# Strassen products for ff tiles 16 to 19 in the feed-forward blocks of a decoder layer, on one Trainium2 core

## The chip, the cores and the metric

One core of one Trainium2 chip runs the whole kernel. The metric is device microseconds of one execution. TensorE (PE) does the matmuls; its weight loads (PEld) run beside them. VectorE (DVE), ScalarE (ACT) and GpSimd (POOL) do the elementwise work, SyncE (SP) issues most DMAs. Each engine takes its own instructions in order and waits for the others at semaphores.

## What is computed

One decoder layer on 512 tokens of width 1024, all in float32: a feed-forward block, a token mixer of three attention kinds, and a second feed-forward block. Each of them takes an RMS-normalised input. The change touches the feed-forward blocks (FFN 1 and FFN 2) alone:

```python
def swiglu(x, w_gate, w_up, w_down):
    return (jax.nn.silu(x @ w_gate) * (x @ w_up)) @ w_down

x = x + 0.5 * swiglu(rms_norm(x, ffn1_norm[i]), ffn1_w_gate[i], ffn1_w_up[i], ffn1_w_down[i])
x = x + token_mixer(rms_norm(x, mix_norm[i]), w_in[i], ...)
x = x + 0.5 * swiglu(rms_norm(x, ffn2_norm[i]), ffn2_w_gate[i], ffn2_w_up[i], ffn2_w_down[i])
```

The inner width D_FF is 2816, which is 22 ff tiles of 128.

## The kernel before

**Products in parts.** Every float32 operand is split into a high part in the matmul's own number format (ACT, a copy) and a low part, the rest (DVE or POOL, a subtraction). A product is three matmuls: high x high, high x low, low x high (`mm3`, L502). For weights the two parts are `whi` (L106, ACT) and `wlo` (L107). A matmul streams 512 columns.

**Weights.** `Weights` (L61) holds a list of loads (`specs`) and a list of halves to be split (`plan`), in order of use. `get` splits up to the half that is asked for. `bg`, called once for each step of work, splits the half two places ahead of the current one. `sub` is the engine that does `wlo`: DVE in the feed-forward blocks. After the last half of a load is split, the load two further on is issued on SP. Split halves live in four rotating buffers, or in tiles of their own where `W.held` (L397) names them.

**Gate and up.** `ffn` (L564) runs 11 steps p, each for two ff tiles (2p and 2p+1): g0, g1 (gate), u0, u1 (up). Each of these is 24 matmuls (`mm_in`). Gate results go through tanh on ACT and into `m` on DVE (`act_g`), up results are multiplied to `a` on DVE (`act_u`).

**Down, as Strassen products.** For ff tiles 0 to 15, four tiles (512 rows of `w_down`) make a block. Block c's left operands come from the steps 2c and 2c+1 (`left_blocks`): four quarter sums on POOL for the second tile of a pair, split on ACT and DVE after the next gate or up half (`split_sums`: `sh` and `sl`, then one more split of half that size). Block c's seven products are made in steps 2c+2 and 2c+3, one behind each gate or up half (`down_block`): 12 matmuls each, into one PSUM bank of each of two kinds, and added on DVE into the residual x (`add_x`, L644), each bank at one or two places. The right operands come from `Blocks` (L127): two loads of 1 MB, a sum on POOL ahead of the first product and one behind each of the splits 1 to 4; the splits' `wlo` of these seven are always POOL's. The next block is loaded when part 6 is split.

**Down, plain.** ff tiles 16 to 21 are split as they are (`ah`, `al`). In step 10 tiles 16 and 17 (`d4`) come between gate and up: 48 matmuls. After step 10 the tail multiplies tiles 18 to 21 (`d5_0`, `d5_1`): for each of four token tiles two halves of 12 matmuls, each added into x (`down_tile`).

**The tail of FFN 1** carries the norm of the mixer in three stages over the following token tiles (`Stages`, `tick`): square and sum on ACT, a power on POOL (`pow`, the operation `nr1..r`, L519), `h` on DVE in two halves (L534: x times `pow` times gain), eight transposes on PE (`nt`, L543), and their split into `hmh` (ACT) and `hml` (DVE). In a tick the transposes and split of tile t-1 are issued ahead of the square of tile t. `W.bg(4)` in each round splits one of the four parts c0.0 to c1.1 (128 x 912) of the first mixer weights. The c tile (24 matmuls of 456 columns) follows on PE. The tail of FFN 2 has no norm; it writes each half tile of the output (256 KB) through SP.

Of the kernel before, what the change touches and what calls it, by code (L numbers as in the profile page):

```python
# [12 lines left out]
F32R = mybir.dt.float32r  # L13
# [7 lines left out]
NT = SEQ // 128  # L21
# [212 lines left out]
def drain(g):  # L234
    for _ in g:
        pass
# [8 lines left out]
def hybrid_trunk_kernel(ctx: ExitStack, tc: tile.TileContext, x, rel_bias, ffn1_norm, ffn1_w_gate, ffn1_w_up,  # L245
# [3 lines left out]
    nc = tc.nc  # L249
# [24 lines left out]
    def t4(name, dt=F32):  # L274
        return big.tile([128, 1024], dt, tag="t4", name=name)

    def t4k(name):
        return t4(name, F32R).rearrange("p (k t) -> p k t", k=2)
# [9 lines left out]
    specs, plan, blocks = [], [], {}  # L288

    def add_spec(loads, parts, name, planned=True):  # L290
        specs.append((loads, parts, name))
        if planned:
            plan.extend((name, p) for p in range(len(parts)))

    def cols(w, name, c0, planned=True):

        def view(raw):
            return raw.rearrange("p (k c) -> p k c", k=8)
        add_spec([(view, w[:, c0:c0 + 256].rearrange("(k p) c -> p k c", p=128))],
                 [lambda raw, g=g: view(raw)[:, :, g * 128:g * 128 + 128] for g in range(2)], name, planned)  # L300
# [8 lines left out]
    def rows(w, name, r0, nk, c0, nc_):  # L309

        src = w[r0:r0 + nk * 128, c0:c0 + nc_].rearrange("(k p) c -> p k c", p=128)
        loads = [(lambda raw: raw[:, :nk * nc_].rearrange("p (k c) -> p k c", k=nk), src)]
        parts = [lambda raw, h=h: raw[:, :nk * nc_].rearrange("p (k c) -> p k c", k=nk)
                 [:, h * nk // 2:(h + 1) * nk // 2, :] for h in range(2)]
        add_spec(loads, parts, name)

    def ffn_specs(f):
        wg, wu, wd = ffn_w[f]
        for c in range(4):
            src = wd[c * 512:c * 512 + 512].rearrange("(k p) c -> p k c", p=128)  # L320
            blocks[f"w{f}{c}"] = Blocks(
                nc, lambda h, c=c: big2.tile([128, 4, 512], F32, tag="hT", name=f"raww{f}{c}{h}"),
                lambda c=c: t4(f"rawe{f}{c}").rearrange("p (k c) -> p k c", k=2),
                [src[:, :, h * 512:h * 512 + 512] for h in range(2)],
                lambda c=c: c < 3 and blocks[f"w{f}{c + 1}"].load())
        for p in range(11):
            between = p in range(2, 10)
            cols(wg, f"g{f}{p}", 256 * p, not between)
            if p == 10:
                rows(wd, f"d{f}4", 16 * 128, 2, 0, 1024)  # L330
            cols(wu, f"u{f}{p}", 256 * p, not between)
            if between:
                for i, (kind, j) in enumerate((("g", 0), ("g", 1), ("u", 0), ("u", 1))):
                    plan.append((f"{kind}{f}{p}", j))
                    if p % 2 * 4 + i < 7:
                        plan.append((f"w{f}{p // 2 - 1}", p % 2 * 4 + i))
        for h in range(2):
            rows(wd, f"d{f}5_{h}", (18 + 2 * h) * 128, 2, 0, 1024)

    ffn_specs(0)  # L340
    def c_view(raw):
# [52 lines left out]
        rows(w_out, f"wo{n}", 256 * n, 2, 0, 1024)  # L394
    ffn_specs(1)
    W = Weights(nc, rawp, wsp, specs, plan, blocks, 2)
    W.held, W.held_tile = [(n, p) for n in ("d05_0", "d15_0", "wo2", "c0") for p in range(2)], lambda name: t4(name, F32R)  # L397


    xt = [t4(f"x{t}") for t in range(NT)]  # L400
# [101 lines left out]
    def mm3(ps, terms):  # L502

        n = len(terms)
        for i, (lh, ll, rh, rl) in enumerate(terms):
            for q, (l, r) in enumerate(((lh, rh), (lh, rl), (ll, rh))):
                nc.tensor.matmul(ps, l, r, start=i == 0 and q == 0, stop=i == n - 1 and q == 2)  # L507
                if q == 2 or ps.shape[1] == 512:
                    yield ps.shape[1] * (1 if ps.shape[1] == 512 else 3) / 2400
# [37 lines left out]
    def hk(hT, k, s):  # L547
        return hT[k // 4][0][:, k % 4, s], hT[k // 4][1][:, k % 4, s]

    ALL = slice(0, SEQ)  # L550

    def tok(t):
        return slice(t * 128, (t + 1) * 128)
# [10 lines left out]
    def ffn(f, hT, order, hooks, after_tile):  # L564
# [3 lines left out]
        def mm_in(kind, p, j, ps, s):  # L568
            wh, wl = W.get(f"{kind}{f}{p}", j)
            for k, _ in enumerate(mm3(ps[:, s], [(wh[:, k, :], wl[:, k, :]) + hk(hT, k, s) for k in range(KD)])):  # L570
                if p == 10 and kind == "u" and k % 12 == 0 or p and k == 0:
                    W.bg(4 if p == 10 else 2)

        def act_g(ff, g):
            th = tmp.tile([128, 512], F32, tag="z", name=f"th{f}{ff}")
# [5 lines left out]
        def act_u(ff, m, u):  # L581
            a = tmp.tile([128, 512], F32, tag="p", name=f"a{f}{ff}", bufs=6)
            nc.vector.tensor_tensor(a, m, u, op=ALU.mult)  # L583
            if ff < 16:
                left_blocks(ff, a)
                return
            if ff % 2 == 0:
                aT[ff // 2, "pair"] = (t4k(f"ah{f}{ff}"), t4k(f"al{f}{ff}"))
            pair = aT[ff // 2, "pair"]
            aT[ff] = (pair[0][:, ff % 2, :], pair[1][:, ff % 2, :])  # L590
            split(aT[ff][0], aT[ff][1], a)
# [41 lines left out]
        def down_block(c, i):  # L633

            w = W.get(f"w{f}{c}", i)
            W.bg()
            for u in range(2):
                ps = (mm, sc)[u](f"dn{f}{c}{i}{u}")
                drain(mm3(ps, [left(c, pr, i, u) + (w[0][:, pr, :], w[1][:, pr, :]) for pr in range(2)]))
                for hr, hc, sign in INTO[i]:  # L640
                    add_x(ps, 2 * hr + u, HALVES[hc], sign)
# [4 lines left out]
        def down_tile(t, k0, parts, hook=None):  # L646
            for half in range(2):
                ps = sc(f"dn{f}{k0}{half}{t}")
                csl = slice(512 * half, 512 * half + 512)
                terms = []  # L650
                for k, w in enumerate(parts):
                    ah, al = aT[k0 + k]
                    terms.append((ah[:, tok(t)], al[:, tok(t)], w[0][:, 0, csl], w[1][:, 0, csl]))
                drain(mm3(ps, terms))
                if half == 0 and hook is not None:
                    hook()
                add_x(ps, t, csl)

        for p in range(11):
            ps, ms = {}, {}  # L660
            step = 0
            if p == 1:
                blocks[f"w{f}0"].load()
            W.cap = W.first[f"u{f}0", 1] if p == 0 else 1 << 30
            todo = order if p == 0 else [("g", 0, ALL), ("g", 1, ALL), None, ("u", 0, ALL), ("u", 1, ALL)]
            for item in todo:
                if item is None:
                    if p == 10:
                        parts = [W.get(f"d{f}4", k) for k in range(2)]
                        for t in range(NT):  # L670
                            if t % 2 == 0:
                                W.bg()
                            down_tile(t, 16, parts)
                    continue
                if callable(item):
                    item()
                    continue
                kind, j, s = item
                if (kind, j) not in ps:
                    ps[kind, j] = (mm if kind == "g" else sc)(f"{kind}{f}{p}{j}")  # L680
                mm_in(kind, p, j, ps[kind, j], s)
                while late:
                    late.pop()()
                if p == 0 and s.stop == SEQ:
                    W.cap += 1
                    W.split(W.cap)
                if s.stop == SEQ:
                    if kind == "g":
                        ms[j] = act_g(2 * p + j, ps["g", j])
                    else:  # L690
                        act_u(2 * p + j, ms[j], ps["u", j])
                if p in range(2, 10):
                    if p % 2 * 4 + step < 7:
                        down_block(p // 2 - 1, p % 2 * 4 + step)
                    step += 1
            if p in hooks:
                hooks[p]()
        parts = [W.get(f"d{f}5_{k // 2}", k % 2) for k in range(4)]
        for t in range(NT):
            down_tile(t, 18, parts, nstage.tick)  # L700
            after_tile(t)
            nstage.tick()
            W.bg(4)


    nstage = Stages()
# [18 lines left out]
    def u_part(f, p):  # L725
# [4 lines left out]
    order = [n0(1, 2), n0(0, 3), ("g", 0, lo2), n0(2, 2), n0(1, 3), u_part(0, 0), ("g", 1, lo2), n0(2, 3), u_part(0, 1),  # L730
             ("u", 0, lo2)] + rest
# [683 lines left out]
    for n in range(2):  # L1415
        parts = [W.get(f"wo{n}", p) for p in range(2)]
# [3 lines left out]
    parts = [W.get(f"wo{2 + k // 2}", k % 2) for k in range(4)]  # L1420
# [45 lines left out]
```

## Time and profile before

| | |
|---|---|
| runs | 1292.51, 1290.85, 1292.12 us |
| median | 1292.12 us |
| the profiled execution | 1292.1 us |
| its span, first to last instruction | 1290.0 us |
| mean granted clock of TensorE | 0.994 of full speed |
| PE busy in the span | 99% |

The profile is of one execution. A row of a timeline tells when an instruction (or several alike in a row, x2) began and how long it took; in brackets stands how long its engine had been idle and what released it. An operation that has begun but cannot get its operands counts as running. The ends of matmuls are modelled, so the distance of two starts is the better measure of one.

### The profile page before, as it was taken

To read this page: it belongs to the slowest core of one execution; us is meant where nothing else is said; L and a number is where in the kernel's file an instruction comes from. 1 tells how busy PE (TensorE), PEld (TensorE's weight loads), DVE (VectorE), ACT (ScalarE), POOL (GpSimd) and SP (SyncE) were. 2 spreads that over 40 slices of the span, in tenths; PEclk is the share of its full clock that TensorE was granted. 3 is DMA by queue.
4 is the path that set the end of the run, shared out by engine and by line. 5 is a ranking of instruction groups with operands and counts; after the bars stand their busy time and mean duration, and the time that the engine had idled before them with its cause. 6 is when DMAs were issued, how large, how long until landed. Compare 5 with 4: busy or idle time off the path is not lost. (4 is left out here: it accounts for less than half of the span.)

```text
span 1290.0 us, 17385 instructions
## 1 busy us (share of the span) xinstructions
PE 1273.0 (99%) x6880; PEld 1081.7 (84%) x6880; DVE 798.7 (62%) x1377; ACT 484.1 (38%) x872; POOL 475.8 (37%) x313
## 2 busy tenths in 40 slices
PE   9999999999999999999999999999999999999998
PEld 8888888888889889889887778888898888888887
DVE  4467777765573766597854554446645767676553
ACT  4242333332243555454556432224233333333220
POOL 2475757561011444446440000000015756666500
PEclk9999999999999999999989999999999999999999
DMA  5424141422433222222221034433332233333131
GB/s 196 141 69 139 57 162 37 161 69 82 137 126 96 60 81 79 87 66 83 66 83 46 33 103 147 131 96 101 98 108 89 98 99 102 112 108 103 66 98 66
DMA packets 101779, 125.08 MB, mean 97 GB/s; under 512 B 3817, under 2 KB 85225, under 8 KB 101698
## 3 DMA queue, kind: packets, MB, share of 16 engines
q1 hardware_dynamic: 96690, 114.08, 27.2%
q10 hardware_dynamic: 3456, 5.24, 1.3%
q0 software_dynamic: 1552, 4.65, 1.1%
q8 instruction: 54, 0.88, 0.3%
q14 instruction: 27, 0.22, 0.1%
HBM read 119.13 MB, written 4.84 MB: 96 GB/s over the span
## 5 line engine op out<-in xcount | busy, mean ns | idle before, releaser
L107 DVE TENSOR_TENSOR wlo<-raw,whi 128x1024 fp32r<-128x1024 f32 (+1 forms) x146 | 219.7, 1510 | 61.3 <-ACT whi L106 61.0
L106 ACT ACTIVATE whi<-raw 128x1024 fp32r<-128x1024 f32 (+1 forms) x178 | 185.5, 1050 | 64.8 <-PE u L507 26.5
L644 DVE SCALAR_TENSOR_TENSOR x<-dn,x 128x512 f32<-128x512 f32 x224 | 143.4, 682 | 30.0 <-PE dn L507 27.5
L107 POOL TENSOR_TENSOR wlo<-raww,whi 128x1024 fp32r<-128x1024 f32 x40 | 99.5, 2487 | 96.6 <-ACT whi L106 96.6
L583 DVE TENSOR_TENSOR a<-m,u 128x512 f32<-128x512 f32 x44 | 30.2, 687 | 101.8 <-PE u L507 101.8
L107 POOL TENSOR_TENSOR wlo<-raw,whi 128x1024 fp32r<-128x1024 f32 x32 | 76.7, 2395 | 29.0 <-ACT whi L106 25.1
L576 ACT ACTIVATE th<-g 128x512 f32<-128x512 f32 x44 | 26.2, 595 | 143.2 <-PE g L507 143.1
L507 PE MATMUL gt<-rmh,wlo 128*128 128x512 f32 x192 | 76.2, 397 | 0.0
L507 PE MATMUL gt<-rml,whi 128*128 128x512 f32 x192 | 76.0, 396 | 0.0
L507 PE MATMUL gt<-rmh,whi 128*128 128x512 f32 x192 | 76.0, 396 | 0.0
L507 PE MATMUL g<-hah,whi 128*128 128x512 f32 (+1 forms) x192 | 71.6, 373 | 0.2 <-ACT hah L512 0.2
L507 PE MATMUL g<-hal,whi 128*128 128x512 f32 (+1 forms) x192 | 71.4, 372 | 0.3 <-DVE hal L513 0.3
L507 PE MATMUL g<-hah,wlo 128*128 128x512 f32 (+1 forms) x192 | 71.4, 372 | 0.1
L507 PE MATMUL u<-hbh,wlo 128*128 128x512 f32 (+1 forms) x192 | 71.4, 372 | 0.0
L507 PE MATMUL u<-hah,wlo 128*128 128x512 f32 (+1 forms) x192 | 71.4, 372 | 0.0
L507 PE MATMUL g<-hbh,whi 128*128 128x512 f32 (+1 forms) x192 | 71.4, 372 | 0.0
L507 PE MATMUL u<-hah,whi 128*128 128x512 f32 (+1 forms) x192 | 71.4, 372 | 0.0
L507 PE MATMUL u<-hbh,whi 128*128 128x512 f32 (+1 forms) x192 | 71.4, 372 | 0.0
L507 PE MATMUL g<-hbl,whi 128*128 128x512 f32 (+1 forms) x192 | 71.3, 372 | 0.0
L507 PE MATMUL g<-hbh,wlo 128*128 128x512 f32 (+1 forms) x192 | 71.3, 371 | 0.0
L507 PE MATMUL u<-hbl,whi 128*128 128x512 f32 (+1 forms) x192 | 71.3, 371 | 0.0
L507 PE MATMUL u<-hal,whi 128*128 128x512 f32 (+1 forms) x192 | 71.3, 371 | 0.0
(1111 smaller groups left out, 3493.3 us busy)
## 6 DMA issues: line engine op xcount, KB each, us to landing
raw<-in_w_in SPq DMA_DIRECT2D x25, 1024.0 KB, 5.1
raw<-in_ffn_w_gate SPq DMA_DIRECT2D x22, 1024.0 KB, 5.1
raw<-in_ffn_w_up SPq DMA_DIRECT2D x22, 1024.0 KB, 5.2
raww<-in_ffn_w_down SPq DMA_DIRECT2D x16, 1024.0 KB, 6.1
raw<-in_ffn_w_down SPq DMA_DIRECT2D x6, 1024.0 KB, 5.0
raw<-in_w_in SPq DMA_DIRECT2D x8, 512.0 KB, 4.5
raw<-in_w_out SPq DMA_DIRECT2D x4, 1024.0 KB, 4.9
x<-in_x SPq DMA_DIRECT2D x4, 512.0 KB, 6.2
```

Of the source, the lines that this page charges most:

```text
L106: nc.scalar.activation(h, src, AF.Copy)
L107: sub.tensor_tensor(l, src, h.bitcast(F32), op=ALU.subtract)
L507: nc.tensor.matmul(ps, l, r, start=i == 0 and q == 0, stop=i == n - 1 and q == 2)
L576: nc.scalar.activation(th, g, AF.Tanh, scale=0.5)
L583: nc.vector.tensor_tensor(a, m, u, op=ALU.mult)
L644: nc.vector.scalar_tensor_tensor(xt[t][:, csl], ps, 0.25 * sign, xt[t][:, csl], op0=ALU.mult, op1=ALU.add)
```

## The change

The four ff tiles 16 to 19 become a fifth Strassen block. Its left operands come from steps 8 and 9 as with the other blocks; its seven products all fall into step 10, two behind g0, two behind g1, two behind u0 and one behind u1 (`products`). The plan lists the halves in that order. `d4` and its 48 matmuls go away, and the tail multiplies ff tiles 20 and 21 alone, 6 matmuls for each half of a token tile. Fewer tiles are held apart: `d5` is split into the rotating buffers. `mm_in` calls `bg` once in every step, also in the tenth. While the tail runs, `W.sub` is POOL, so that the parts c0.0 to c1.1 are split there; behind the tail it is DVE again.

```diff
+    def products(p, i):
+
+        if p == 10:
+            return range(2 * i, min(2 * i + 2, 7))
+        return range(p % 2 * 4 + i, min(p % 2 * 4 + i + 1, 7))
+
     def ffn_specs(f):
         wg, wu, wd = ffn_w[f]
-        for c in range(4):
+        for c in range(5):
...
-                lambda c=c: c < 3 and blocks[f"w{f}{c + 1}"].load())
+                lambda c=c: c < 4 and blocks[f"w{f}{c + 1}"].load())
         for p in range(11):
-            between = p in range(2, 10)
+            between = p > 1
             cols(wg, f"g{f}{p}", 256 * p, not between)
-            if p == 10:
-                rows(wd, f"d{f}4", 16 * 128, 2, 0, 1024)
             cols(wu, f"u{f}{p}", 256 * p, not between)
             if between:
                 for i, (kind, j) in enumerate((("g", 0), ("g", 1), ("u", 0), ("u", 1))):
                     plan.append((f"{kind}{f}{p}", j))
-                    if p % 2 * 4 + i < 7:
-                        plan.append((f"w{f}{p // 2 - 1}", p % 2 * 4 + i))
-        for h in range(2):
-            rows(wd, f"d{f}5_{h}", (18 + 2 * h) * 128, 2, 0, 1024)
+                    plan.extend((f"w{f}{p // 2 - 1}", q) for q in products(p, i))
+        rows(wd, f"d{f}5", 20 * 128, 2, 0, 1024)
...
-    W.held, W.held_tile = [(n, p) for n in ("d05_0", "d15_0", "wo2", "c0") for p in range(2)], lambda name: t4(name, F32R)
+    W.held, W.held_tile = [(n, p) for n in ("wo2", "c0") for p in range(2)], lambda name: t4(name, F32R)
...
-                if p == 10 and kind == "u" and k % 12 == 0 or p and k == 0:
-                    W.bg(4 if p == 10 else 2)
+                if p and k == 0:
+                    W.bg()
...
-            if ff < 16:
+            if ff < 20:
                 left_blocks(ff, a)
...
-            todo = order if p == 0 else [("g", 0, ALL), ("g", 1, ALL), None, ("u", 0, ALL), ("u", 1, ALL)]
+            todo = order if p == 0 else [("g", 0, ALL), ("g", 1, ALL), ("u", 0, ALL), ("u", 1, ALL)]
             for item in todo:
-                if item is None:
-                    if p == 10:
-                        parts = [W.get(f"d{f}4", k) for k in range(2)]
-                        for t in range(NT):
-                            if t % 2 == 0:
-                                W.bg()
-                            down_tile(t, 16, parts)
-                    continue
...
-                if p in range(2, 10):
-                    if p % 2 * 4 + step < 7:
-                        down_block(p // 2 - 1, p % 2 * 4 + step)
+                if p > 1:
+                    for q in products(p, step):
+                        down_block(p // 2 - 1, q)
                     step += 1
...
-        parts = [W.get(f"d{f}5_{k // 2}", k % 2) for k in range(4)]
+        parts = [W.get(f"d{f}5", k) for k in range(2)]
+        W.sub = nc.gpsimd
         for t in range(NT):
-            down_tile(t, 18, parts, nstage.tick)
+            down_tile(t, 20, parts, nstage.tick)
             after_tile(t)
             nstage.tick()
             W.bg(4)
+        W.sub = nc.vector
```

## Rows read from the trace of the kernel before

**Rows 1.** The page: the span, and its part 1 (busy us, share of the span, instructions of each engine).
```profile
span 1290.0 us, 17385 instructions
PE 1273.0 (99%) x6880; PEld 1081.7 (84%) x6880; DVE 798.7 (62%) x1377; ACT 484.1 (38%) x872; POOL 475.8 (37%) x313
```
**Rows 2.** The chain that ended last, in order of time (start us, us, what), its last 75 us: a `down_block` product of step 9, the two plain ff tiles in the middle of step 10, the tail of FFN 2, the last add.
```profile
1215.37 2.72 PE dn L507 x12
1242.57 10.88 PE dn L507 x48
1264.33 21.83 PE dn L507 x96
1286.17 0.69 DVE x L644
```
**Rows 3.** Timeline of PE around the tail of FFN 1 (start us, us, engine, line, operation, out<-in, count [idle before <-releaser]): the first matmul of the tail, the transposes `nt` of tiles 0 to 2, the first matmul of the c tile, and a weight load of the c tile that waited.
```profile
344.74 0.39 PE L507 MATMUL dn<-whi,ah 128*128 128x512 f32 x1
355.63 1.03 PE L543 MATMUL nt<-ident,h 128*128 128x128 f32 x8
361.96 1.03 PE L543 MATMUL nt<-ident,h 128*128 128x128 f32 x8
368.30 1.03 PE L543 MATMUL nt<-ident,h 128*128 128x128 f32 x8
369.09 0.45 PE L507 MATMUL c<-whi,hmh 128*128 128x456 f32 x1
373.10 0.19 PEld L507 LDWEIGHTS c<-wlo,hmh 128*128 128x128 f32 x1 [0.22 <-DVE wlo L107]
```
**Rows 4.** Timelines of DVE, ACT and POOL in the tail of FFN 1 (columns as above): `a` and `ah` of ff tile 21; the last add of token tile 0 and its `pow`; `whi`, `pow`, `wlo` and `h` of token tile 1.
```profile
344.94 0.69 DVE L583 TENSOR_TENSOR a<-m,u 128x512 f32<-128x512 f32 x1 [0.74 <-PE u L507]
345.67 0.63 ACT L512 ACTIVATE ah<-a 128x512 fp32r<-128x512 f32 x1 [2.91 <-DVE a L583]
350.38 0.69 DVE L644 SCALAR_TENSOR_TENSOR x<-dn,x 128x512 f32<-128x512 f32 x1 [2.03 <-PE dn L507]
352.52 0.56 POOL L519 TENSOR_TENSOR nr10r<-nr10v,neghalf 128x1 f32<-128x1 f32 x1 [52.52 <-DVE nr10v L517]
358.27 0.97 ACT L106 ACTIVATE whi<-raw 128x912 fp32r<-128x912 f32 x1
358.65 0.55 POOL L519 TENSOR_TENSOR nr11r<-nr11v,neghalf 128x1 f32<-128x1 f32 x1 [5.57 <-DVE nr11v L517]
359.27 1.11 DVE L107 TENSOR_TENSOR wlo<-raw,whi 128x912 fp32r<-128x912 f32 x1 [0.70 <-ACT whi L106]
360.30 1.41 DVE L534 SCALAR_TENSOR_TENSOR h<-x,nr11r,gain 128x512 f32<-128x512 f32 x2
```
**Rows 5.** DMA issues, from the page's part 6 and from the last 26 us (out<-in, queue, count, KB each, median us from issue to landing).
```profile
raww<-in_ffn_w_down SPq DMA_DIRECT2D x16, 1024.0 KB, 6.1
out_x<-x SPq DMA_DIRECT2D x8, 256.0 KB, 2.0
```
**Rows 6.** Timelines of DVE and POOL at two places (columns as above): in the mixer a pair of `work` operations alone and one with a POOL split, then 10 us of FFN 2 in step 7.
```profile
438.14 1.34 DVE L1070 SCALAR_TENSOR_TENSOR work<-rl,cw,work 128x384 f32<-128x384 f32 x2 [0.68 <-ACT rl L1069]
446.95 3.28 DVE L1070 SCALAR_TENSOR_TENSOR work<-rl,cw,work 128x384 f32<-128x384 f32 x2 [0.77 <-ACT rl L1069]
447.29 2.52 POOL L107 TENSOR_TENSOR wlo<-raw,whi 128x1024 fp32r<-128x1024 f32 x1
1140.19 2.40 POOL L107 TENSOR_TENSOR wlo<-raww,whi 128x1024 fp32r<-128x1024 f32 x1
1140.45 3.22 DVE L107 TENSOR_TENSOR wlo<-raw,whi 128x1024 fp32r<-128x1024 f32 x1
1142.54 3.38 POOL L150 TENSOR_TENSOR raww<-raww,raww 128x1024 f32<-128x1024 f32 x1
1143.59 3.42 DVE L513 TENSOR_TENSOR sl<-sum,sh 128x1024 fp32r<-128x1024 f32 x1
1146.31 2.95 POOL L107 TENSOR_TENSOR wlo<-raww,whi 128x1024 fp32r<-128x1024 f32 x1 [0.38 <-ACT whi L106]
1146.93 2.88 DVE L513 TENSOR_TENSOR a<-a,a 128x512 fp32r<-128x512 f32 x1
```
**Rows 7.** The chain in order of time and the timelines of DVE, POOL and ACT at the start of step 8 in FFN 2, where products of the third block begin.
```profile
1169.12 5.44 PE g L507 x24
1169.77 1.22 DVE L107 TENSOR_TENSOR wlo<-raw,whi 128x1024 fp32r<-128x1024 f32 x1
1169.93 2.35 POOL L600 TENSOR_TENSOR sum<-a,a 128x256 f32<-128x256 f32 x2 [1.31 <-DVE a L583]
1173.00 1.06 ACT L512 ACTIVATE sh<-sum 128x1024 fp32r<-128x1024 f32 x1 [5.92 <-POOL sum L600]
1173.05 0.74 POOL L600 TENSOR_TENSOR a<-a,a 128x256 f32<-128x256 f32 x1
```
**Rows 8.** PE in four stretches of 3.4 us (stretch: us, PE busy us (matmuls), granted clock as a share of full speed, DMA share, GB/s).
```profile
571.46:574.87 3.41, 1.82 (x13) 1.00 0.47 166
574.87:578.29 3.42, 3.42 (x19) 0.50 0.02 5
687.51:690.93 3.42, 2.06 (x17) 1.00 0.14 40
690.93:694.34 3.41, 3.41 (x25) 1.00 0.00 0
```

## Prediction

> **What bounds the kernel now.** I read the page first: PE is busy 1273.0 of 1290.0 us, DVE 62%, ACT 38%, POOL 37% [rows 1]. Then the chain in order of time: its last 75 us are PE without a hole, a `down_block` product (12 matmuls) taking 2.72 us, so 0.2267 us a matmul [rows 2]. A matmul less is worth that, as long as nothing else becomes late. So I read, engine by engine, the two places where the change shortens PE's work between two dependent steps: the last gate and up step, and the loop over four token tiles behind it. In FFN 1 that loop carries the next norm: 344.74 to 369.09 is 24.35 us for 4 x 24 matmuls (21.76) and 3 x 8 transposes (0.79 each), 24.13 us of work [rows 3]. PE waits 0.2 us there, but the norm is only just in time: the second half of `h` of tile 1 ends at 360.30 + 1.41 = 361.71, its transposes start at 361.96 [rows 3, 4].
>
> **1. Matmuls.** Before, the four ff tiles cost 48 matmuls (10.88 us) in the middle of step 10 and half of the 96 at the end (21.83 us) [rows 2]. After it there are 7 products x 12 = 84 and a tail of 48: 132 for 144. 12 x 0.2267 = 2.72 us less per FFN, **-5.44 us** for two.
>
> **2. Work beside PE.** Per FFN there are 24 + 8 adds into x for 16: 16 x 0.69 = 11 us more on DVE; POOL gets 7 splits and 5 sums of 2.4 us and 10 sums of 0.74 us, some 36 us in a step of 38 us. Most of it has room: a product's four adds take 2.7 us, and PSUM has three buffers for each kind. As bare time I cost it at nothing. The loads are 3 MB either way (two 1 MB loads of block 4 for `d4` and half of `d5`); block 4's load is issued when the last part of block 3 is split, 19 us ahead of its first product as with the blocks before, and lands 6.1 us later [rows 5]. On SP it stands ahead of u10's load, as block loads do in every other step. What is not free is a port that DVE and POOL share.
>
> **3. DVE and POOL shut each other out.** At 1140 to 1150 us six operations stand in strict turn: POOL's split ends at 1142.59, then DVE's `wlo` runs its 1.1 us (recorded 3.22), then POOL's sum to 1145.92, DVE's `sl` to 1147.01 (recorded 3.42), POOL's split to 1149.26, and then DVE's `a`, 2.88 us long for an operation of 0.69 [rows 6]. All have both inputs in SBUF. When one ends, the engine that was waiting goes next, even where the other has another operation ready behind it. The DVE form of `h` behaves so too: two SCALAR_TENSOR_TENSOR of SBUF inputs take 1.34 us alone and 3.28 where a POOL split arrived during the first [rows 6].
> The Trainium skill (SBUF — State Buffer, section Who interferes with whom) says that whoever issues first gets the pair for the whole instruction and the other blocks fully. It does not say who is next when both have more. If DVE kept the pair for its next instruction, the sum below would be that of rival 3, about 1291.4; the rows speak for turns.
>
> **4. A wait before the second gate of step 10, new.** Count from the start of g10's first half, after the same place in step 8 (1169.12) [rows 7]. Two products now follow it, so POOL has its next split queued right behind the four left sums of ff 19. Those started at +0.81 and took 4 x 0.72, plus 0.9 behind a DVE `wlo` that this place no longer has; so they end at +3.7 and POOL splits product 1 until +6.1. ACT's `sh` ends at +4.1 (0.9 sooner than in the rows); DVE's `sl` waits until 6.1, runs to 7.3; POOL's sum to 9.7; DVE's second left split to 10.3; POOL's split of product 2 to 12.6; only then DVE's `wlo` for the second half of g10, ready at 13.8. PE is through the first half and the two products at 5.44 + 2 x 2.72 = 10.88 and needs that `wlo` in its third matmul, at 11.3. Wait 2.5 us per FFN, **+5.0 us**. Before, these `wlo` were split a whole half step ahead. Bounds: 0 per FFN (DVE keeps the port for `sl` and its successor: ready at 9.5 to 11.4) to 2.7. I take 2.5, by the six rows in turn.
>
> **5. Start of the tail.** `d5` is split two places ahead, its second part at the start of the last product. From the end of u10: `a` 0.20 to 0.89, `ah` to 1.56 [rows 4], then `whi` (1.05) to 2.55 and DVE's `wlo` (1.2) to 3.8. PE needs it behind the product and 4 matmuls, at 2.72 + 0.91 = 3.6. **+0.4 us** for both FFNs.
>
> **6. The tail of FFN 1.** A tile is now 12 matmuls, 2.72 us; with its neighbour's 8 transposes PE has 3.51 us of work a round. The chain that must fit in: add, square on ACT, `pow` on POOL, `h` on DVE, transposes, `hmh` on ACT, and behind that, in ACT's order, the next square. Tile 0: matmuls end at 344.74 + 24 x 0.2267 = 350.18 and `pow` at 353.08, so +2.90 [rows 3, 4]. The c weights' `wlo` moves from DVE (1.11, ahead of `h`) to POOL, where 912 columns take 2.40 x 912 / 1024 = 2.14. Its `whi` ends at 359.24, `pow` at 359.20 [rows 4]: so `h`'s first half starts, POOL's split arrives under 0.1 us later and waits, and takes the port between the halves. First half to +3.65, POOL to +5.8, second half to +6.4, the last 4 transposes to +6.85: 3.3 us idle. The next rounds, from the end of transposes (356.42): `pow` ends at +2.78 (359.20), first half +3.5, POOL +5.65, second half +6.25, transposes +6.7: 3.2 us idle, twice. Together 9.7, less the 0.2 of before: **+9.5 us**. Lower bound, if `h` is never parted: 2.90 or 2.78 + 1.41 + 0.45, so 1.3 + 1.1 + 1.1 less 0.2, +3.3. I take the upper one, by the 3.28 us row.
> Queued behind the waiting half on DVE are the next tile's two adds, and ACT's next square waits for those; that is inside the round.
>
> **7. c1's last part.** Its `wlo` follows `pow` and `h`'s first half of tile 3 on POOL: +2.78 + 0.7 + 2.14 = +5.65 from the start of the c tile; PE asks for it at +3.8 (373.10 less the 0.22 it waited, less 369.09) [rows 3]. Wait 1.85 for 0.22: **+1.6 us** (+1.0 if `h` is not parted).
>
> **8. The tail of FFN 2.** No norm hangs on it. Outputs of 256 KB come every 1.36 us instead of 2.72 and land in 2.0 us [rows 5]; the last add and output stay as long as they are. 0.
>
> **9. Clock.** In one stretch PE was busy 1.82 of 3.41 us, and the granted clock was 0.5 (1.2 GHz) in the next; behind another with 2.06 of 3.42 it stayed at 1.0 [rows 8]. A fall costs 1.7 us where PE sets the pace (3.4 us at half speed). With a wait of 2.5 us in step 10 PE is idle for longer than in either, but it may fall across two such stretches: 0 to 2 falls, 0 to 3.4 us; I take one, **+1.7 us**. In the tail PE waits anyhow and a fall costs little.
>
> **Sum.** -5.44 + 5.0 + 0.4 + 9.5 + 1.6 + 1.7 = +12.8 us. The profiled execution took 1292.1 us (span 1290.0), the median is 1292.12; so **1304.9 us**.
>
> **Rivals.**
> 1. `h` is not parted: the split of the c weights reaches POOL too late to matter, or DVE's second half goes first. -5.44 + 5.0 + 0.4 + 3.3 + 1.0 + 1.7 = +6.0, 1298.1 us. For it: `h` has never met a POOL split in this trace. Against it: same form of instruction, same order of arrival as in [rows 6].
> 2. No wait before g10's second half, because `sl` passes before POOL's split: -5.44 + 0.4 + 9.5 + 1.6 = +6.1, 1298.2 us. For it: 0.3 us decide whether `sl` or POOL's split is first. Against it: POOL's split has its inputs early.
> 3. Neither: -5.44 + 0.4 + 3.3 + 1.0 = -0.7, 1291.4 us, no change.
> 4. Faster: as 3, and the norm's round fits into PE's too. The place is the tail of FFN 1; the round would have to be under some 4.0 us for a gain over 2.6. It needs that the next tile's square need not wait for `hmh`; the 6.1 us from transposes to the end of the next `h` before (355.63 to 361.71, 1.0 of it the DVE `wlo`) speak against it. -5.44 + 0.4 + 1.0 + 1.0 = -3.0, 1289 us.
> 5. Worse: two falls of the clock and one in the tail that reaches the c tile: +3.4 more, 1308.3 us.
>
> **How the numbers follow.** Forecast 0.47; rivals 0.17, 0.16, 0.09, 0.06 and 0.05. About 0.2% (2.6 us) is what a measurement of this kernel can tell from no change. Slower: 0.47 + 0.17 + 0.16 + 0.05 = 0.85; same 0.09; faster 0.06. The range leaves out rivals 3 and 4 and takes the first two with 2 us to spare, above to rival 5: 1296 to 1308.5.
>
> **What would show it.** PE: 24 dn matmuls less; a hole of 2 to 3 us in g10's second half in both FFNs, with a DVE `wlo` as releaser; in FFN 1's tail `h` recorded as one half of 0.7 and one of nearly 3 us, with a POOL `wlo<-raw` of 912 columns in between, transposes 6.7 us apart; the c tile waiting on POOL. If `h` takes 1.41 us for the pair, step 6 is wrong; if g10 runs through, step 4. If the total is under 1290 us, the norm's round was not what PE waits for, and the reading of the tail fails.

## The result and the profile after

The changed kernel takes 1300.85 us in the median (1299.82 to 1302.79, 6 runs), the kernel before 1291.39 us (1290.41 to 1292.51, 6 runs): ratio 1.0074, 95% interval [1.0061, 1.0087], 9.5 us slower. The forecast was 1304.9, in a range of 1296 to 1308.5. The profiled execution took 1300.9 us, with a span of 1299.1, against 1292.1 and 1290.0.

The page's first part, which answers to [rows 1]:

```profile
span 1299.1 us, 17463 instructions
PE 1268.0 (98%) x6856; PEld 1073.5 (83%) x6856; DVE 840.8 (65%) x1401; ACT 494.0 (38%) x882; POOL 564.9 (43%) x361
```

PE has 24 matmuls less and is busy 5.0 us less, yet the span is 9.1 us longer. So PE waits. The view of PE's waits (waiting for what: us in total, times, the longest) names whom it waits for. None of these three is in that view of the kernel before, where the c tile lost 0.22 us at a weight load [rows 3]:

```profile
PE nt L545 <- DVE h L536: 6.5, 5, 1.9
PE g L509 <- DVE wlo L107: 3.9, 2, 1.9
PE c L509 <- POOL wlo L107: 1.4, 1, 1.4
```

**The second gate half of step 10.** Timelines of PE, DVE and POOL in FFN 1 (columns as in [rows 3]):

```profile
325.46 0.50 PE L509 MATMUL g<-hah,wlo 128*128 128x512 f32 x1 [1.93 <-DVE wlo L107]
...
316.15 3.13 DVE L515 TENSOR_TENSOR sl<-sum,sh 128x1024 fp32r<-128x1024 f32 x1 [3.32 <-ACT sh L514]
319.19 2.89 DVE L515 TENSOR_TENSOR a<-a,a 128x512 fp32r<-128x512 f32 x1
322.01 0.68 DVE L580 SCALAR_TENSOR_TENSOR m<-th,g 128x512 f32<-128x512 f32 x1
322.61 2.80 DVE L107 TENSOR_TENSOR wlo<-raw,whi 128x1024 fp32r<-128x1024 f32 x1
...
315.80 2.39 POOL L107 TENSOR_TENSOR wlo<-raww,whi 128x1024 fp32r<-128x1024 f32 x1
318.15 3.38 POOL L150 TENSOR_TENSOR rawe<-raww,raww 128x1024 f32<-128x1024 f32 x1
321.50 2.83 POOL L107 TENSOR_TENSOR wlo<-raww,whi 128x1024 fp32r<-128x1024 f32 x1
```

Read by their ends, in turn: POOL's split ends at 318.19, `sl` at 319.28, POOL's sum at 321.53, DVE's `a` at 322.08, POOL's split at 324.33, DVE's `wlo` at 325.41. DVE's three operations on two SBUF inputs are recorded with 2.8 to 3.1 us where they take 1.22, 0.68 and 1.22 us alone ([rows 7], and E2 below). PE's matmul on that `wlo` follows at 325.46. Counted from the start of g10's first half (311.94) these six ends lie at +6.2, 7.3, 9.6, 10.1, 12.4 and 13.5 us; step 4 had them at +6.1, 7.3, 9.7, 10.3, 12.6 and 13.8. FFN 2 has the same wait, and there it stands on the chain that ended last (start us, us, what):

```profile
1235.45 5.45 PE u L509 x24
1240.93 0.70 DVE a L585
1241.69 2.13 POOL sum L602 x3
1243.85 1.07 ACT sh L514
1244.94 3.13 DVE sl L515
1248.07 2.81 DVE a L515
1250.88 0.60 DVE m L580
1251.47 2.74 DVE wlo L107
1254.25 5.29 PE g L509 x22
...
1284.96 10.28 PE dn L509 x44
1295.27 0.69 DVE x L646
```

Where the chain was PE alone [rows 2], it now leaves PE for 13 us and comes back through the `wlo`. Two of that half's 24 matmuls ran ahead of the wait.

**The tail of FFN 1.** Timelines of POOL, DVE and PE in the second round and at the c tile, which answer to [rows 3, 4]:

```profile
367.02 0.55 POOL L521 TENSOR_TENSOR nr11r<-nr11v,neghalf 128x1 f32<-128x1 f32 x1 [3.26 <-DVE nr11v L519]
367.68 2.69 POOL L107 TENSOR_TENSOR wlo<-raw,whi 128x912 fp32r<-128x912 f32 x1
...
361.04 3.27 DVE L536 SCALAR_TENSOR_TENSOR h<-x,nr10r,gain 128x512 f32<-128x512 f32 x2 [0.67 <-POOL nr10r L521]
367.61 3.32 DVE L536 SCALAR_TENSOR_TENSOR h<-x,nr11r,gain 128x512 f32<-128x512 f32 x2 [0.67 <-POOL nr11r L521]
374.22 3.27 DVE L536 SCALAR_TENSOR_TENSOR h<-x,nr12r,gain 128x512 f32<-128x512 f32 x2 [0.66 <-POOL nr12r L521]
...
361.85 0.66 PE L545 MATMUL nt<-ident,h 128*128 128x128 f32 x4 [0.86 <-DVE h L536]
364.37 0.66 PE L545 MATMUL nt<-ident,h 128*128 128x128 f32 x4 [1.86 <-DVE h L536]
383.63 0.48 PE L509 MATMUL c<-wlo,hmh 128*128 128x456 f32 x1 [1.44 <-POOL wlo L107]
```

The pair of halves of `h` takes 3.27 to 3.32 us for the 1.41 of [rows 4], and the eight transposes fall into four and four, in the first and third round with a wait ahead of each, in the second with one ahead of the latter four alone. The POOL split was queued 0.07 us behind the start of `h` and got its turn between the halves. The rounds (start to start of `h`) are 6.57 and 6.61 us long.

**By stretches.** For all kernels the same five distances, from the starts of PE's matmuls: FFN 1's first gate to its last up matmul (all 11 steps but the last product); from there to the first matmul of the c tile (the tail); the c tile's start to the `iq` tile behind it; and in FFN 2 the 11 steps and what is left to PE's end.

| us | FFN 1, 11 steps | FFN 1, tail | c to iq | FFN 2, 11 steps | FFN 2, tail |
|---|---|---|---|---|---|
| before | 331.78 | 24.57 | 21.71 | 328.52 | 22.20 |
| after | 339.65 | 25.90 | 23.31 | 336.29 | 14.31 |
| E1 | 339.69 | 23.46 | 23.16 | 336.28 | 14.31 |
| E2 | 337.60 | 26.62 | 23.39 | 333.98 | 14.36 |
| E3 | 339.65 | 20.30 | 21.61 | 336.28 | 14.31 |
| E6 | 337.41 | 23.74 | 21.68 | 334.01 | 14.33 |
| E5 | 331.78 | 25.70 | 23.32 | 328.52 | 22.17 |
| E4 | 331.84 | 24.59 | 21.72 | 334.01 | 14.33 |

After less before: +7.87, +1.33, +1.60, +7.77, -7.89, together +10.7. Of the 1.6 us that are missing to the 9.1 of the spans, 1.3 lie in the mixer, from the `iq` tile to FFN 2's first gate (544.6 us before, 543.3 after), where the profiled execution before has a fall of the clock at a place at which the one after has none (below); 0.3 lie ahead of FFN 1's first gate.

### The profile page after: what moved, and what is told of

The parts are those of the page before. It is cut to its first block, busy times and chain, and to the rows that moved or that the text cites. A ratio compares the mean times of both kernels' runs of the same rounds, so it can differ in the third digit from the quotient of the medians.

```text
span 1299.1 us, 17463 instructions
## 1 busy us (share of the span) xinstructions
PE 1268.0 (98%) x6856; PEld 1073.5 (83%) x6856; DVE 840.8 (65%) x1401; ACT 494.0 (38%) x882; POOL 564.9 (43%) x361
## 5 line engine op out<-in xcount | busy, mean ns | idle before, releaser
L107 DVE TENSOR_TENSOR wlo<-raw,whi 128x1024 fp32r<-128x1024 f32 x134 | 214.7, 1606 | 58.4 <-ACT whi L106 57.4
L106 ACT ACTIVATE whi<-raw 128x1024 fp32r<-128x1024 f32 (+1 forms) x170 | 178.0, 1050 | 72.8 <-PE u L509 34.6
L646 DVE SCALAR_TENSOR_TENSOR x<-dn,x 128x512 f32<-128x512 f32 x256 | 161.8, 682 | 12.6 <-PE dn L509 10.2
L107 POOL TENSOR_TENSOR wlo<-raww,whi 128x1024 fp32r<-128x1024 f32 x50 | 126.0, 2520 | 98.8 <-ACT whi L106 98.7
L107 POOL TENSOR_TENSOR wlo<-raw,whi 128x1024 fp32r<-128x1024 f32 (+1 forms) x36 | 87.3, 2425 | 29.7 <-ACT whi L106 25.3
L509 PE MATMUL dn<-whi,a 128*128 128x512 f32 x240 | 78.8, 389 | 0.0
L602 POOL TENSOR_TENSOR sum<-a 128x256 f32<-128x256 f32 x40 | 29.4, 736 | 111.5 <-DVE a L585 89.9
```

Of the source, the lines that this page charges most:

```text
L106: nc.scalar.activation(h, src, AF.Copy)
L107: sub.tensor_tensor(l, src, h.bitcast(F32), op=ALU.subtract)
L602: plus = lambda out, l, r, op=ALU.add: nc.gpsimd.tensor_tensor(out, l, r, op=op)
L646: nc.vector.scalar_tensor_tensor(xt[t][:, csl], ps, 0.25 * sign, xt[t][:, csl], op0=ALU.mult, op1=ALU.add)
```

## The experiments

The theory is that of the prediction: the change loses at two places, each by DVE and POOL taking turns (the wait in step 10, steps 3 and 4; `h` parted in the tail, steps 6 and 7). Its rival: the added work of DVE and POOL and the norm's own order set these places, so that an edit only moves the waits. Times are given as a ratio to the kernel before in the same session (median 1290.8 or 1290.9 us, 18 and 21 runs), with its 95% interval, and in us by that ratio; a difference to the changed kernel (+9.5) is taken between two such ratios and is good to 2.0 to 2.4 us (two half intervals of 0.09 to 0.13%, added as squares), so the traces decide what is smaller.

**E1: the low parts of the c weights stay with DVE in the tail** (the changed kernel else).

```diff
-        W.sub = nc.gpsimd
         for t in range(NT):
...
-        W.sub = nc.vector
```

> The changed kernel, but in the tail the low parts of c0.0 to c1.1 stay with DVE, as in the kernel before. Theory (the round of the tail is set by the POOL split that parts DVE's pair of halves of h, and c1's wait by the same split): the pair is whole again, 1.3 to 1.5 us recorded instead of 3.27, but DVE's split of 1.1 us stands ahead of it. From one group of transposes to the next some 6.1 us instead of 6.6, and the hole of 1.44 us in the c tile goes: about 4 us less than the changed kernel, some 1297. Rival (with DVE's split back in front of h the round is no shorter, DVE's order is what bounds it): transposes 6.6 us apart or more, only the c tile's hole goes, 0 to 1.5 us less, or more time than the changed kernel.

Measured: 1297.72 us, 1.0053 [1.0040, 1.0066], 2.7 us less than the changed kernel. Two fences, the timelines of DVE and PE in the second round, and PE's clock at the start of the c tile in stretches (stretch: us, PE busy us (matmuls), granted clock, DMA share, GB/s):

```profile
366.82 1.11 DVE L107 TENSOR_TENSOR wlo<-raw,whi 128x912 fp32r<-128x912 f32 x1 [0.70 <-ACT whi L106]
367.85 1.41 DVE L536 SCALAR_TENSOR_TENSOR h<-x,nr11r,gain 128x512 f32<-128x512 f32 x2
368.74 1.29 PE L545 MATMUL nt<-ident,h 128*128 128x128 f32 x8 [1.80 <-DVE h L536]
374.51 1.29 PE L545 MATMUL nt<-ident,h 128*128 128x128 f32 x8 [1.71 <-DVE h L536]
```

```profile
372.39:375.80 3.41, 1.67 (x11) 1.00 0.35 141
375.80:379.22 3.42, 3.42 (x11) 0.51 0.37 153
```

The pair is whole (1.41), the round 5.77, the tail 2.44 us shorter, PE's wait in the c tile gone. The expected 4 us are there, as 2.44 + 1.44. But c to iq is still 23.16: a fall of the clock to 0.51 (1.2 GHz) lies on the c tile, where PE does not wait and each matmul takes twice as long. The theory holds for the pair, the round and PE's wait; in this profiled execution the clock took back at the c tile what the wait there had cost.

**E2: the seven products of step 10 dealt one, three, two and one** (the changed kernel else; products and their order are the same).

```diff
         if p == 10:
-            return range(2 * i, min(2 * i + 2, 7))
+            return range((0, 1, 4, 6)[i], (1, 4, 6, 7)[i])
```

> The changed kernel with the seven products of step 10 dealt one, three, two and one behind g0, g1, u0 and u1 instead of two, two, two and one. Theory (the wait of 1.93 us at the head of g10's second half, and what PE loses around it, 2.3 to 2.4 us in each FFN, comes from the POOL split and sum of the second product's weights that stand in turn with DVE's sl and wlo): with one product there the wait goes in both FFNs and nothing new comes, 4.8 us less than the changed kernel, some 1296. Rival (the work of step 10 is too much for DVE and POOL wherever it is put): the wait moves behind g1's three products or into u0, a new hole of 1 us or more in each FFN, and the time stays within 1 us of the changed kernel or above it.

Measured: 1296.10 us, 1.0039 [1.0027, 1.0052], 4.5 us less than the changed kernel. DVE and POOL at the place of the wait:

```profile
317.06 1.22 DVE L515 TENSOR_TENSOR sl<-sum,sh 128x1024 fp32r<-128x1024 f32 x1 [3.12 <-ACT sh L514]
318.20 0.68 DVE L515 TENSOR_TENSOR a<-a,a 128x512 fp32r<-128x512 f32 x1
...
319.18 2.41 POOL L107 TENSOR_TENSOR wlo<-raww,whi 128x1024 fp32r<-128x1024 f32 x1 [2.44 <-ACT whi L106]
```

POOL has nothing queued behind the left sums any more, `sl` and `a` pass in their bare times, and the `wlo` of the second gate half is DVE's at 312.72, a half step ahead. PE has no wait in step 10 of either FFN, behind the three products neither: the 11 steps are 2.05 and 2.31 us shorter. The tail of FFN 1 is 0.72 us longer than in the changed kernel: two falls of the clock lie in it or at its end (from 361.73 and from 375.38), where that one has one. Only product 1 has moved, from behind g0 to behind g1, and it does not come late there. The rival falls for step 10.

**E3: the low part of c0 and c1 written as zeros by POOL** (the changed kernel else). This leaves out the low part of those weights; POOL still has an instruction at that place, but one that reads nothing from SBUF.

```diff
+            if name in ("c0", "c1"):
+                nc.gpsimd.memset(l.bitcast(F32), 0.0)
+            else:
-            sub.tensor_tensor(l, src, h.bitcast(F32), op=ALU.subtract)
+                sub.tensor_tensor(l, src, h.bitcast(F32), op=ALU.subtract)
```

> The changed kernel, but the low parts of the mixer weights c0 and c1 are filled with zeros by a POOL memset instead of being worked out from the two SBUF inputs (this leaves out the low part of those weights). Theory (h is parted because POOL's split has two SBUF inputs and takes turns with DVE): the pair of halves of h takes 1.3 to 1.5 us again, transposes some 4.6 us apart instead of 6.6, no hole in the c tile: about 7.6 us less than the changed kernel, some 1293. Rival (the round is set by the order add, square, pow, h, transposes and by ACT, POOL's split only lies beside it): the round stays over 6 us, under 2 us less.

Measured: 1294.48 us, 1.0028 [1.0018, 1.0038], 5.9 us less than the changed kernel by the medians, 7.2 by the two profiled executions (1293.71 and 1300.9). DVE, POOL and PE in the second round:

```profile
365.79 1.42 DVE L539 SCALAR_TENSOR_TENSOR h<-x,nr11r,gain 128x512 f32<-128x512 f32 x2 [0.67 <-POOL nr11r L524]
365.71 0.85 POOL L108 MEMSET wlo<- 128x912 f32 x1
366.69 1.29 PE L548 MATMUL nt<-ident,h 128*128 128x128 f32 x8 [0.73 <-DVE h L539]
```

POOL's instruction lies over the first half of `h`, and `h` is not slowed: a busy POOL alone does not part the pair; the subtraction, which reads SBUF, does. (The memset is also shorter, 0.85 us for a recorded 2.69, and begins 0.08 us ahead of `h` and not behind it; a POOL instruction of the full length that reads nothing was not run.) The Trainium skill (SBUF — State Buffer, section Who interferes with whom) says that a DVE instruction with two SBUF inputs contends with a GpSimd one that reads SBUF and not with one that only writes; this row agrees (1.42 us beside the memset, 3.32 beside the split). Tail and c tile are 5.60 and 1.70 us shorter, rounds 4.7 to 4.8. That is still 1.2 us over PE's 3.5 us of work (0.7 to 0.9 of it recorded as a wait): even with no subtraction for the c weights in it the norm's own chain is longer than PE's work in a round.

**E5: that part of the change alone**, in the kernel before.

```diff
+        W.sub = nc.gpsimd
         for t in range(NT):
             down_tile(t, 18, parts, nstage.tick)
...
+        W.sub = nc.vector
```

> The kernel before with one part of the change alone: while the tail runs, the low parts of c0.0 to c1.1 are POOL's. Theory (POOL's split parts h, so that a round takes 6.6 us whatever PE has to do in it): PE, with 6.2 us of work in a round, waits 0.4 to 0.5 us in each of three rounds, and the c tile waits 1.4 us for c1's last part as in the changed kernel: 2 to 3 us slower than before. Rival (the part is harmless or a gain, since DVE is relieved of four splits ahead of h, and only PE's shorter round makes the tail wait): within 0.7 us of before, or below.

Measured: 1293.27 us, 1.0016 [1.0007, 1.0025], 2.1 us slower than before. PE:

```profile
356.58 0.66 PE L543 MATMUL nt<-ident,h 128*128 128x128 f32 x4 [0.26 <-DVE h L534]
363.32 0.63 PE L543 MATMUL nt<-ident,h 128*128 128x128 f32 x4 [0.18 <-DVE h L534]
375.94 0.48 PE L507 MATMUL c<-wlo,hmh 128*128 128x456 f32 x1 [1.45 <-POOL wlo L107]
```

Under a tail with four ff tiles the parted `h` costs little (tail +1.13), the c tile the same as after the change (+1.61). So this edit is a loss by itself, with nothing to hide behind; the shorter round only makes it larger.

**E6: E1 and E2 together.**

> The changed kernel with both edits: products of step 10 dealt one, three, two and one, and the low parts of c0.0 to c1.1 left with DVE in the tail. Theory (the two prices are in different places and add): 4.8 + 4.0 = 8.8 us less than the changed kernel, some 1292, within 2 us of before. Rival (they are one wait that the other edit finds again): no more than the larger of the two alone, some 1296.

Measured: 1292.61 us, 1.0014 [1.0005, 1.0023], 7.7 us less than the changed kernel where the two alone gave 2.7 and 4.5. The prices add, within what these differences are good for. It is still 1.8 us slower than before, and the table says where: FFN 2 gains (+5.49 - 7.87 = -2.4), FFN 1 loses (+5.63 - 0.83 = +4.8). Either tail has 36 matmuls less, 8.16 us; FFN 2's is shorter by 7.87 us for it, FFN 1's by 0.83.

**E4: the change in FFN 2 alone, dealt as in E2; FFN 1 as before.** `W.sub` stays DVE throughout: the tail of FFN 2 splits no weights for a next stage. The main places of the edit:

```diff
+    def products(p, i):
+        if p == 10:
+            return range((0, 1, 4, 6)[i], (1, 4, 6, 7)[i])
+        return range(p % 2 * 4 + i, min(p % 2 * 4 + i + 1, 7))
...
-        for c in range(4):
+        for c in range(5 if f else 4):
...
-            between = p in range(2, 10)
+            between = p > 1 and (f or p < 10)
...
+        if f:
+            rows(wd, f"d{f}5", 20 * 128, 2, 0, 1024)
...
-            if ff < 16:
+            if ff < (20 if f else 16):
```

> The change in FFN 2 alone, with the products of step 10 dealt one, three, two and one; FFN 1 as in the kernel before, plain d4 and the tail with four ff tiles. Theory (the 12 matmuls saved in an FFN are worth 2.72 us where nothing else becomes late, and in FFN 2 no norm hangs on the tail): 2.5 us less than before, some 1289. Rival (step 10 with seven products costs on DVE and POOL what it saves on PE, or the last outputs come later because they follow each other twice as fast): within 1 us of before, or above.

Measured: 1287.94 us (1287.23 to 1289.72, 11 runs), 0.9977 [0.9968, 0.9985]: 3.0 us faster than before and 12.5 faster than the changed kernel. The chain that ended last, in step 10 and the tail:

```profile
1239.30 5.44 PE g L515 x24
1244.74 8.21 PE dn L515 x36
1252.96 5.44 PE u L515 x24
1258.40 5.44 PE dn L515 x24
1263.84 5.44 PE u L515 x24
1269.28 3.62 PE dn L515 x16
1272.93 10.30 PE dn L515 x44
1283.26 0.69 DVE x L652
```

The chain is PE alone again, through three products in a row (36 matmuls in 8.21 us). The table gives +5.49 - 7.87 = -2.38 us for -2.72 of matmuls.

## Why the prediction came out, step by step

- **Step 1** (matmuls, -5.44): 24 fewer, as counted. E4 shows that those of one FFN are a gain where nothing else becomes late.
- **Step 2** (bare work beside PE, 0): right. In E4 seven products, their splits, sums and adds lie in step 10 with no wait of PE, and 0.34 us of the 2.72 are all that they and the start of the tail cost.
- **Steps 3 and 4** (turns; a wait of 2.5 us in each FFN): 7.87 - 5.44 = 2.43 and 7.77 - 5.44 = 2.33 us, of it 1.93 recorded as a wait (in FFN 1 and in FFN 2). The six ends came as forecast, to 0.4 us, and E2 shows the cause.
- **Step 5** (+0.4 for both): FFN 2's tail lost 7.89 of 8.16 us (36 matmuls), so 0.27 in one FFN.
- **Steps 6 and 7** (+9.5 and +1.6): over its work (the last up matmul, 12 and 48 matmuls and 24 transposes, 16.2 us) the stretch of 25.90 us holds 9.7 us, 0.2 of them step 5's; forecast was 9.7 without those, of which 9.5 were new. The c tile lost 1.60. Round by round, between the starts of PE's matmuls, the tail holds 3.2, 3.2 and 3.1 us more than its work, where 3.3, 3.2 and 3.2 were forecast; the waits recorded are less, 6.5 us, since they count from the modelled end of a matmul and since in the second round matmuls at half the clock (below) fill what would have been a wait. E1, E3 and E5 show the cause, E3 the bound: with `h` whole the tail is 5.60 us shorter.
- **Step 8** (0): right, the last add and the outputs end as before behind PE's end.
- **Step 9** (clock, +1.7): wrong, it came to 0. No fall came behind the wait in step 10, in FFN 1 or 2, after the change or in E1 or E3: six waits of 1.93 us. The two stretches over which it lies in FFN 2 are the last of the rows below. The fall in the tail, which I had costed at little, is there, and it cost nothing: PE's second round, in which it lies, is no longer than the first, and behind it PE still waits 1.26 us for `h`. In E1 a fall reached the c tile and cost 1.5 us, which is rival 5's mechanism.

Without step 9 the steps sum to +11.1 us where the five stretches give +10.7. The measured difference is 9.5. In the two profiled executions the 1.6 us between 10.7 and 9.1 lie outside the five stretches, most of them in the mixer behind the `iq` tile, where the change edits nothing; that the same holds for the other runs is likely but not shown, as there is one trace of each kernel. So the mechanism came out at both places, and the number is 4.0 us too high: 1.7 by step 9, 1.6 because the other steps sum to 11.1 and not 9.5, and 0.7 because the sum starts from 1292.12 where the median of the six runs before is 1291.39. The rivals 1 to 4 fall by the rows of `h` (3.3, not 1.4) and of the wait (1.93, not 0).

## What to carry to other kernels

Count the matmuls saved only where the stage has nothing else in it that must end in order. A tail that carries the next stage's norm had 0.2 us of room, and taking half of its matmuls away uncovered a chain of 4.7 us a round (E3; 5.8 with the c weights' split on VectorE in E1, 6.6 with it on GpSimd); the same edit in the tail without a norm gave 7.9 of its 8.2 us. Before work goes to GpSimd to relieve VectorE, look for what VectorE has just begun at that moment: a GpSimd split that arrives 0.1 us behind a pair of VectorE operations costs the pair 1.9 us (3.3 for 1.41), and four of them cost the kernel more than the four VectorE splits of 1.1 us that they replaced (E5). And the order of independent work is worth a look: which half step the second product stands behind decided 4.5 us (4.4 in the traces of step 10, for both FFNs).

## What was not expected of the hardware

The granted clock of PE in stretches of this kernel (columns as under E1, after the change):

```profile
362.39:365.81 3.42, 1.56 (x11) 1.00 0.00 0
365.81:369.22 3.41, 3.41 (x10) 0.51 0.37 154
1249.85:1253.26 3.41, 2.47 (x11) 1.00 0.00 0
1253.26:1256.68 3.42, 2.43 (x11) 1.00 0.36 91
```

In the tail of FFN 1, where PE had been busy 1.56 of 3.42 us, the next stretch was granted 0.51, that is 1.2 GHz; around the single wait of 1.93 us in step 10 it stayed at 1.00, 2.4 GHz, all six times (both FFNs, after the change and in E1 and E3). Falls came in the tail of FFN 1 or at its end, where waits follow one another: one each after the change, in E1 and in E6, two in E2, but none in E3 and E5, whose tails wait less.

Falls elsewhere were not the same in the profiled executions: before and E4 have one in the mixer at 533.9 and 533.5 us, and the stretch from its `b1q` to its `a1q` tile takes 51.53 and 51.56 us there; the six others have none at that place (five of them have one or two elsewhere in the mixer), and it takes 49.82 to 50.12. Why the two kernels with FFN 1 as it was have it, and E5, whose FFN 1 differs by the splits alone, has not, is left open. It is 1.5 us, as much as several of the terms of the sum, and the mixer from the `iq` tile to FFN 2's first gate, whose code no edit changes, took between 541.8 and 544.6 us in the eight; no term for it can be read off one trace.
